# Compressed attention in chains of two token blocks, with its values laid out once by transfers

## The chip, the cores and the metric

The kernel runs on one core of a Trainium2 chip. The core has a matrix engine (TensorE: PE in the profile, PEld for its weight loads), VectorE (DVE), ScalarE (ACT), GpSimd (POOL) and SyncE (SP, which here only issues transfers). The metric is the device time of one execution in microseconds (us), and the median of several runs is quoted.

## The reference, cut to what matters

The model is a two-layer decoder trunk on 512 tokens. Layer A holds a "native sparse attention" of 12 query heads in 3 groups of 4; the heads of a group share keys and values. Three branches are summed with sigmoid gates: compressed blocks, selected blocks and a sliding window. With 512 tokens every allowed block is selected, so the last two branches are ordinary causal attention with two sets of keys. The change is in the compressed branch:

```
def compress(t, i):                       # 31 blocks of 32 tokens, one every 16
    tb = (t[:, :, blk_tok] + cmp_pos[i]).reshape(B, G, n_cmp, CMP_BLOCK * D)
    return gelu(tb @ cmp_w1[i] + cmp_b1[i]) @ cmp_w2[i] + cmp_b2[i]

k_c = rope(rmsnorm(compress(split_heads(k_cmp, G), 0), k_norm[0]), cmp_end)
v_c = compress(split_heads(v_cmp, G), 1)
...
m_c = cmp_end[None, :] <= t[:, None]      # a block counts once it has ended
p_c = masked_softmax(einsum('bgrqd,bgcd->bgrqc', q_b, k_c) * scale, m_c)
o_c = einsum('bgrqc,bgcd->bgrqd', p_c, v_c)
o_c = where(m_c.any(-1)[:, None], o_c, 0) # the first 31 tokens see no block
...
return g_b[..., 0:1] * o_c + g_b[..., 1:2] * o_s + g_b[..., 2:3] * o_w
```

Each query thus has a softmax over at most 31 compressed keys, padded to 32.

## The kernel before, in words

The 512 tokens are 4 blocks of 128, which lie on the 128 partitions. Layer A is `layer_a`. It first makes the projection that feeds the compression and the gates, and the projection of group 0. Then `attend` walks a list of items. An item is one step of attention with a `front` (score products and softmax) and a `back` (transposing the probabilities and multiplying them with the values), and `back` runs one item late. Between items `attend` takes steps from `work`, a queue of other jobs: the compression itself ("cmp"), the projections of groups 1 and 2, the queries, keys and values of the memory attention, and part of the output projection. How many steps are taken for an item is set per group in `RA`. This gives the order in which the program is written; a scheduler then orders the instructions of each engine by that priority and a simulated time, so instructions of neighbouring items are mixed. Each engine runs its own list strictly in order.

Per group there are 16 items of the two causal branches (`attn_a`: front L1041, back L1081) and 4 items of the compressed branch, one for each token block (`cfront`, `cback`, made by `cmp_scores`). `spread` sets where in the list the 4 stand: in group 0 they are items 9 to 12 in one run; in groups 1 and 2 every second item from the second on.

One compressed item is a chain of small instructions:

- four products of queries with the group's compressed keys into a score tile in PSUM (L985);
- on VectorE, adding mask and low part (L990, L991), the row maximum (L993) and its subtraction (L994); the exponential on ScalarE (L995); on VectorE again the sum (L997), the reciprocal (L998) and the product with the gate (L1003, or L1001 for block 0, which also zeroes the first 31 tokens); the product of probabilities and factor on GpSimd (L1004);
- in `back`, one transpose on the matrix engine (L1009) and its copy from PSUM into `pcT` by `evT` (L741 on VectorE or L743 on ScalarE).

When a group's chains are done, `cmp_out` (L1015) adds the compressed branch to the output of a pair of heads with one product of `pcT` and `VCB`. `VCB` is the group's compressed values, 32 rows by 64, repeated at four places of a 128-partition tile that is zero elsewhere: GpSimd clears the tile (L975) and ScalarE makes four copies (L977), for each group anew in a single buffer. The values `vc` themselves come from `finish(1)` in `compress` (L940).

The score tiles of the chain and those of the causal branches (L1050 to L1066, freed when ScalarE's exponentials L226 have read them) share three PSUM banks; transposes share two. The causal items' maxima are L1056 and L1068, their reciprocals L1076, the scaling of probabilities on GpSimd is L735, the copies of transposes L741 and L743, the value products L747. The projections of groups 1 and 2 (`proj_a`) keep all engines busy besides: products L270 to L272, evacuation L955, L958 and L959, rotary embedding on GpSimd (L537 to L540, L759), splitting (L710, L711), transposes (L768, L778) into the tiles that L774 and L716 to L718 write out.

Of the kernel before, what the change touches and what calls it, by code (L numbers as in the profile page):

```python
# [17 lines left out]
NB = 4  # L18
# [25 lines left out]

RA = (2.0, 1.16, 1.46, 1.96)
RB = (1.58, 1.85, 1.49, 2.4, 1.9)


# [130 lines left out]
class K:  # L181
# [602 lines left out]
    def layer_a(self):  # L784
        nc, ins = self.nc, self.ins
        xg = self.xg0
        ab = self.t("ab", [P, 768])
        gt = ab[:, 0:144].rearrange("p (b g) -> p b g", b=NB)
        KC = self.c("KC", [P, 3, 2, 32], F32R)
        vc = ab[0:96, 144:208]  # L790
        raw0, st = [], []

        def evac0(b, ps):
            t = self.t("x", [P, 384])
            nc.scalar.activation(t, ps[:, 0:384], AF.Copy, scale=st[0][:, b : b + 1])
            raw0.append(t)
            nc.scalar.activation(gt[:, b, :], ps[:, 384:420], AF.Copy, scale=st[0][:, b : b + 1])
            if b < NB - 1:
                return
            ga = ab[:, 0:144]  # L800
            nc.vector.tensor_scalar(out=ga, in0=ga, scalar1=-1.0, scalar2=80.0, op0=ALU.mult, op1=ALU.min)
            nc.scalar.activation(ga, ga, AF.Exp)
            nc.vector.tensor_scalar(out=ga, in0=ga, scalar1=1.0, scalar2=None, op0=ALU.add)
            nc.vector.reciprocal(out=ga, in_=ga)

        ga, kf, qm, kk, oT, om = [[] for _ in range(3)], [], [], [], [], []
        x0 = self.x

        def hook(k):
            if k + 1 < KT:  # L810
                self.xpart(k + 1)
            i = self.square(k, x0[k], nc.vector)
            if k == KT // 2:
                self.constants_in(i)
            if k == KT - 1:
                self.setup2()
                st.extend(self.stats_cols())
                self.ms = self.mem_stats()

        self.xpart(0)  # L820
        p0 = self.proj_a(
            0, xg, st, ga[0], banks=[self.pacc] * 2 + [self.pS] * 2, lo="v", fine=True, hook=hook
        )
        for _ in range(KT):
            next(p0)
        drain(weave(p0, self.proj(xg, ins["w_a0"], 420, evac0, lo="g", pool=[self.pS, self.pacc, self.pacc, self.pS]), RC[0]))
        e = st[1]
        hidden, finish = self.compress(raw0, KC, vc)
        cmp = dict(KC=KC, vc=vc)
        work, seen, self.kf1 = Work(), [], []  # L830
        comp = chain(hidden(0, self.pacc), weave(hidden(1, self.pacc), finish(0), RC[1]), finish(1))
        work.add(weave(comp, self.mem_kv_whole(0, kf), RC[2]), "cmp")
        work.add(self.proj_a(1, xg, st, ga[1]), "g1")
        work.add(self.proj_a(2, xg, st, ga[2]), "g2", lambda: seen.count(0) == 20)
        work.add(self.mem_q(0, xg, ins["w_am"], e, qm), None, lambda: seen.count(1) == 20)
        work.add(self.mem_keys(0, kf, kk), "mem")
        work.add(self.mem_kv(1, self.kf1))
        work.add(self.outpart(oT, 0, 4, ins["w_ao"], ins["xT"], 0))
        L, C = zip(*[self.attn_a(g, ga[g], gt, cmp, oT) for g in range(3)])
        M = self.mem_items(kf, qm, kk, om, 3, "mem")  # L840
        items = spread(L[0], C[0], 8, 0) + spread(L[1], C[1], 1, 1) + spread(L[2], C[2], 1, 1) + M
        slow = Work()
        slow.add(paced(self.adds, PA), None, lambda: len(seen) >= 12)
        attend(items, work, slow, RA, seen)
        while work.step() is not END:
            pass
        drain(self.outpart(oT + om, 4, 8, ins["w_ao"], None, 4))

    def compress(self, raw0, KC, vc):

        nc, ins = self.nc, self.ins
        acc = {}
# [34 lines left out]
        def finish(which):  # L887
# [48 lines left out]
            else:  # L936
                ps = self.ps(self.pT, [96, HD])
                for kt in range(2):
                    nc.tensor.matmul(ps, gT[:, kt, :], w2[:, kt, :], start=kt == 0, stop=kt == 1)
                nc.vector.tensor_tensor(out=vc, in0=ps, in1=b2, op=ALU.add)  # L940
            yield
        return hidden, finish

# [25 lines left out]
    def cmp_scores(self, g, q4, cmp, gt):  # L969


        nc = self.nc
        KC, vc = cmp["KC"], cmp["vc"]
        VCB = self.t("vcb", [P, 2, P])
        nc.gpsimd.memset(VCB, 0.0)  # L975
        for q in range(4):
            nc.scalar.activation(  # L977
                VCB[32 * q : 32 * q + 32, q // 2, (q % 2) * HD : (q % 2 + 1) * HD], vc[32 * g : 32 * g + 32, :], AF.Copy
            )
        pcT = self.t("x", [P, S])  # L980

        def front(i):
            Sc = self.ps(self.pS, [P, 4, 2, 32])
            for h in range(4):
                nc.tensor.matmul(  # L985
                    Sc[:, h].rearrange("p t c -> p (t c)"), q4[h // 2][:, h % 2, i * P : (i + 1) * P],
                    KC[:, g].rearrange("p t c -> p (t c)"), start=True, stop=True,
                )
            s = self.t("cs", [P, 4, 32])
            nc.vector.tensor_tensor(out=s, in0=Sc[:, :, 0], in1=bcast(self.ccm[:, i, :], 1, 4), op=ALU.add)  # L990
            nc.vector.tensor_tensor(out=s, in0=Sc[:, :, 1], in1=s, op=ALU.add)  # L991
            m = self.t("c1", [P, 4])
            nc.vector.tensor_reduce(out=m, in_=s, axis=AX.X, op=ALU.max)  # L993
            nc.vector.tensor_tensor(out=s, in0=s, in1=bcast(m, 2, 32), op=ALU.subtract)  # L994
            nc.scalar.activation(s, s, AF.Exp)  # L995
            z = self.t("c2", [P, 4])
            nc.vector.tensor_reduce(out=z, in_=s, axis=AX.X, op=ALU.add)  # L997
            nc.vector.reciprocal(out=z, in_=z)  # L998
            gc = gt[:, i, :].rearrange("p (h b) -> p h b", b=3)[:, 4 * g : 4 * g + 4, 0]
            if i == 0:  # L1000
                nc.vector.scalar_tensor_tensor(out=z, in0=z, scalar=self.zc, in1=gc, op0=ALU.mult, op1=ALU.mult)  # L1001
            else:
                nc.vector.tensor_tensor(out=z, in0=z, in1=gc, op=ALU.mult)  # L1003
            nc.gpsimd.tensor_tensor(out=s, in0=s, in1=bcast(z, 2, 32), op=ALU.mult)  # L1004
            return s

        def back(i, s):
            pt = self.ps(self.pT, [P, P])
            nc.tensor.transpose(pt, s.rearrange("p h c -> p (h c)"), self.idf)  # L1009
            self.evT(pcT[:, i * P : (i + 1) * P], pt)  # L1010

        return VCB, pcT, front, back

# [6 lines left out]
    def attn_a(self, g, ga, gt, cmp, out):  # L1020
# [9 lines left out]

        def cback(i, s):
            cs[3](i, s)
            if i == NB - 1:
                cs.append(True)
                close()

# [44 lines left out]
        def back(pr, half, hp, ii, p):  # L1081
# [40 lines left out]
        need = f"g{g}" if g else None  # L1122
        return (
            [Item(front, back, a, g, need) for a in order],
            [Item(cfront, cback, (i,), g, "cmp") for i in range(NB)],
        )

    def outpart(self, oT, k0, k1, wsrc, xsrc, w0, wide=1):
# [692 lines left out]
```

## Time and profile before

| | |
|---|---|
| median of 3 runs | 1273.14 us (1271.8 to 1274.15) |
| the profiled execution: time, span | 1268.89 us, 1267.1 us |
| granted TensorE clock | 0.998 of full speed |
| busy share of the span | PE 98%, PEld 80%, DVE 66%, ACT 59%, POOL 27% |
| instructions | PE 6416, DVE 1516, ACT 1668, POOL 448 |
| chains of the compressed branch | 12, from 105.99 us (first L985) to 244.9 us (last L1009) |

The span is what the profile covers; the time lies 1.79 us above it. A line number stands for the line of the kernel that issued the instruction, and can be that of a helper. In a row of the timeline the first number is the start and the second the duration in us; a bracket at the end gives the idle time of the engine just before and the instruction that ended it.

### The profile page before, as it was taken

How to read it: one execution, taken by the hardware profiler on the slowest of the kernel's cores; microseconds unless marked ns; L12 is line 12 of the kernel's file. 1: busy time of each engine (PE TensorE's matmuls, PEld its weight loads, DVE VectorE, ACT ScalarE, POOL GpSimd, SP SyncE). 2: the span in 40 equal slices, each digit the busy share in tenths (PEclk: the TensorE clock that was granted, in tenths of full speed). 3: DMA queues.
4: the chain of work that ended last, by engine and by line, in shares of the span. 5: the costliest groups of instructions: out<-in, count | busy, mean ns of one | idle time of the engine just before them, and what ended most of it. 6: DMA issues, size and time to landing. Idle time of an engine off the chain costs nothing.

```text
span 1267.1 us, 18289 instructions
## 1 busy us (share of the span) xinstructions
PE 1238.2 (98%) x6416; PEld 1019.6 (80%) x6416; DVE 835.9 (66%) x1516; ACT 750.7 (59%) x1668; POOL 343.1 (27%) x448
## 2 busy tenths in 40 slices
PE   9999989899999999999999999999999999999998
PEld 7768777677788888888888898987788888888887
DVE  6846676755656557566579567787766756656566
ACT  6845578774575364453647457788666445364462
POOL 4546675632040010000002788552222000000000
PEclk9999999999999999999999999999999999999999
DMA  7531241335488697896976331210459789696534
GB/s 266 198 112 65 68 132 61 67 76 135 157 250 239 225 274 220 268 242 216 282 205 190 120 101 58 63 47 9 117 190 277 220 271 241 219 279 204 164 102 164
DMA packets 61835, 215.26 MB, mean 170 GB/s; under 512 B 6736, under 2 KB 14928, under 8 KB 61232
## 3 DMA queue, kind: packets, MB, share of 16 engines
q1 hardware_dynamic: 50656, 143.69, 34.2%
q0 software_dynamic: 9344, 35.77, 14.2%
q10 hardware_dynamic: 1744, 34.63, 7.6%
q8 instruction: 51, 0.84, 0.3%
q14 instruction: 40, 0.33, 0.1%
HBM read 208.83 MB, written 72.35 MB: 222 GB/s over the span
## 4 chain that ended last, share of the span: by engine, by line
PE 80%; DVE 7%; ACT 7%; POOL 2%; issue 2%; DMA 2%; ACTq 0%; POOLq 0%; DVEq 0%
PE s_ps L270 13%; PE s_ps L271 13%; PE s_ps L272 13%; PE s_acc L270 6%; PE s_acc L271 6%; PE s_acc L272 6%; PE s_po L747 3%; PE s_pt L270 3%; PE s_pt L272 3%; PE s_pt L271 3%; ACT s_p L226 1%; DVE s_w L265 1%; PE s_acc L880 1%; PE s_acc L579 1%; PE s_pt L1100 1%
## 5 line engine op out<-in xcount | busy, mean ns | idle before, releaser
L265 DVE TENSOR_TENSOR s_w<-s_st,s_w 128x1024 fp32r<-128x1024 f32 (+3 forms) x254 | 291.0, 1151 | 260.5 <-ACT s_w L263 250.8
L263 ACT ACTIVATE s_w<-s_st 128x1024 fp32r<-128x1024 f32 (+4 forms) x260 | 251.5, 970 | 182.4 <-PE s_pt L272 45.9
L270 PE MATMUL s_ps<-s_act,s_w 128*128 128x512 f32 x568 | 222.0, 393 | 1.1 <-ACT s_act L305 0.7
L271 PE MATMUL s_ps<-s_act,s_w 128*128 128x512 f32 x568 | 221.1, 390 | 0.0
L272 PE MATMUL s_ps<-s_act,s_w 128*128 128x512 f32 x568 | 221.0, 390 | 0.0
L270 PEld LDWEIGHTS s_ps<-s_act,s_w 128*128 128x128 f32 x568 | 106.5, 188 | 24.4 <-ACT s_act L305 1.6
L271 PEld LDWEIGHTS s_ps<-s_act,s_w 128*128 128x128 f32 x568 | 106.7, 188 | 22.9 <-issue 0.8
L272 PEld LDWEIGHTS s_ps<-s_act,s_w 128*128 128x128 f32 x568 | 106.6, 188 | 22.1
L226 ACT ACTIVATE s_p<-s_ps 128x512 f32<-128x512 f32 x64 | 38.2, 598 | 117.9 <-PE s_ps L272 117.1
L270 PE MATMUL s_acc<-s_w,s_act 128*128 128x512 f32 (+3 forms) x288 | 101.4, 357 | 2.3 <-ACT s_sq L518 1.5
L271 PE MATMUL s_acc<-s_w,s_act 128*128 128x512 f32 (+3 forms) x288 | 101.2, 354 | 0.2 <-DVE s_w L265 0.2
L272 PE MATMUL s_acc<-s_w,s_act 128*128 128x512 f32 (+3 forms) x288 | 100.4, 354 | 0.0
L1183 POOL DMA_DIRECT2D sum<-in_w_db_dram x16 | 14.4, 900 | 291.1 <-ACT s_p L226 287.5
L735 POOL TENSOR_SCALAR s_p<-s_p,s_cr,s_ab 128x128 f32<-128x128 f32 (+3 forms) x96 | 61.1, 673 | 55.3 <-DVE s_cr L1076 28.5
L226 ACT ACTIVATE s_p<-s_ps,s_nm 128x256 f32<-128x256 f32 (+3 forms) x128 | 65.6, 523 | 16.4 <-DVE s_nm L726 5.0
L270 PEld LDWEIGHTS s_acc<-s_w,s_act 128*128 128x128 f32 x288 | 54.7, 190 | 8.7 <-ACT s_sq L518 2.5
L743 ACT ACTIVATE s_pt<-s_pt 128x512 f32<-128x512 f32 (+2 forms) x101 | 53.0, 528 | 13.6 <-PE s_pt L1100 6.0
L305 ACT ACTIVATE s_qk<-s_p 128x256 fp32r<-128x256 f32 (+1 forms) x96 | 46.9, 489 | 21.1 <-DVE s_p L1193 19.2
L271 PEld LDWEIGHTS s_acc<-s_w,s_act 128*128 128x128 f32 x288 | 54.8, 190 | 4.7 <-DVE s_w L265 0.4
L272 PEld LDWEIGHTS s_acc<-s_w,s_act 128*128 128x128 f32 x288 | 54.7, 190 | 4.3
L1183 POOL DMA_DIRECT2D sum<-sum x16 | 14.1, 883 | 151.0 <-issue 39.2
L308 DVE TENSOR_TENSOR s_qk<-s_p,s_qk 128x256 fp32r<-128x256 f32 (+1 forms) x96 | 50.0, 520 | 0.7 <-ACT s_qk L305 0.6
(332 smaller groups left out, 2869.3 us busy)
## 6 DMA issues: line engine op xcount, KB each, us to landing
s_st<-in_w_up_dram SPq DMA_DIRECT2D x64, 512.0 KB, 4.3
s_st<-sum SPq DMA_DIRECT2D x64, 512.0 KB, 6.7
s_st<-in_w_db_dram SPq DMA_DIRECT2D x48, 512.0 KB, 4.5
sum<-in_w_db_dram POOLq DMA_DIRECT2D x16, 1024.0 KB, 14.1
sum<-sum POOLq DMA_DIRECT2D x16, 1024.0 KB, 11.0
s_st<-in_w_bq_dram SPq DMA_DIRECT2D x16, 384.0 KB, 3.1
s_st<-in_w_ag_dram SPq DMA_DIRECT2D x11, 512.0 KB, 3.4
s_w<-in_w_c_dram SPq DMA_DIRECT2D x8, 512.0 KB, 4.4
```

The source lines that it names most:

```text
L226: return lambda *a, **k: self.marks.append(f(*a, **k))
L263: nc.scalar.activation(w[:, 0], st, AF.Copy)
L265: e.tensor_tensor(out=w[:, 1], in0=st, in1=w[:, 0], op=ALU.subtract)
L270: mm(ps, lh[0], rh[0], start=start, stop=False, skip_group_check=again)
L271: mm(ps, lh[0], rh[1], start=False, stop=False, skip_group_check=again)
L272: mm(ps, lh[1], rh[0], start=False, stop=stop, skip_group_check=again)
L305: nc.scalar.activation(dst[:, 0], src, AF.Copy)
L308: nc.vector.tensor_tensor(out=dst[:, 1], in0=src, in1=dst[:, 0], op=ALU.subtract)
L735: self.nc.gpsimd.tensor_scalar(out=p, in0=p, scalar1=c, scalar2=g, op0=ALU.mult, op1=ALU.mult)
L743: self.turned = self.nc.scalar.activation(dst, src, AF.Copy)
L747: i = self.nc.tensor.matmul(*a, **k)
L1183: self.behind(self.nc.gpsimd.dma_start(t[o], x, accum_op=ALU.add, max_dma_last_dim=4096))
```

## The change

1. A chain takes two token blocks: 2 chains per group in place of 4. Its score tile is [128, 2, 4, 2, 32], 512 numbers wide (a whole PSUM bank), and each VectorE, ScalarE and GpSimd instruction of the chain covers 256 columns, not 128. The products (now 8 per chain) and the transposes (2 per chain, into one PSUM tile) stay as many in all; the copy into `pcT` is one for two blocks.
2. The zeroing of the first 31 tokens moves from each group's first chain to the gates, in one instruction for all groups.
3. `VCB` holds all three groups. It is cleared once, and right behind `vc` in `finish(1)` twelve small transfers, issued by GpSimd, write the values to their places. The four copies per group on ScalarE and the clearing per group go.
4. Items and ratios: there are 18 items per group, no longer 20, so `RA` is raised to take about as many steps of work per group, the thresholds that start two jobs become 18, and the chains of groups 1 and 2 stand as every third item.
5. `VCB` (three times as large) and the wider chain tiles take more SBUF; the area reserved for GpSimd's transfer descriptors is set to 8192 bytes, which had been left at the default.

```diff
-RA = (2.0, 1.16, 1.46, 1.96)
+RA = (2.22, 1.29, 1.62, 1.96)
...
             nc.vector.reciprocal(out=ga, in_=ga)
+            g0 = gt[:, 0, :].rearrange("p (h k) -> p h k", k=3)[:, :, 0]
+            nc.vector.tensor_scalar(out=g0, in0=g0, scalar1=self.zc, scalar2=None, op0=ALU.mult)
...
-        hidden, finish = self.compress(raw0, KC, vc)
-        cmp = dict(KC=KC, vc=vc)
+        VCB = self.t("vcb", [P, 3, 2, P])
+        nc.gpsimd.memset(VCB, 0.0)
+        hidden, finish = self.compress(raw0, KC, vc, VCB)
+        cmp = dict(KC=KC, VCB=VCB)
...
-        work.add(self.proj_a(2, xg, st, ga[2]), "g2", lambda: seen.count(0) == 20)
-        work.add(self.mem_q(0, xg, ins["w_am"], e, qm), None, lambda: seen.count(1) == 20)
+        work.add(self.proj_a(2, xg, st, ga[2]), "g2", lambda: seen.count(0) == 18)
+        work.add(self.mem_q(0, xg, ins["w_am"], e, qm), None, lambda: seen.count(1) == 18)
...
-        items = spread(L[0], C[0], 8, 0) + spread(L[1], C[1], 1, 1) + spread(L[2], C[2], 1, 1) + M
+        items = spread(L[0], C[0], 8, 0) + spread(L[1], C[1], 1, 2) + spread(L[2], C[2], 1, 2) + M
...
                 nc.vector.tensor_tensor(out=vc, in0=ps, in1=b2, op=ALU.add)
+                for g in range(3):
+                    for q in range(4):
+                        d = VCB[32 * q : 32 * q + 32, g, q // 2, (q % 2) * HD : (q % 2 + 1) * HD]
+                        s_ = vc[32 * g : 32 * g + 32, :]
+                        nc.gpsimd.dma_start(d, s_)
...
-        KC, vc = cmp["KC"], cmp["vc"]
-        VCB = self.t("vcb", [P, 2, P])
-        nc.gpsimd.memset(VCB, 0.0)
-        for q in range(4):
-            nc.scalar.activation(
-                VCB[32 * q : 32 * q + 32, q // 2, (q % 2) * HD : (q % 2 + 1) * HD], vc[32 * g : 32 * g + 32, :], AF.Copy
-            )
+        KC = cmp["KC"]
+        VCB = cmp["VCB"][:, g]
         pcT = self.t("x", [P, S])

         def front(i):
-            Sc = self.ps(self.pS, [P, 4, 2, 32])
-            for h in range(4):
...
+            Sc = self.ps(self.pS, [P, 2, 4, 2, 32])
+            for b in range(2):
+                blk = slice((2 * i + b) * P, (2 * i + b + 1) * P)
+                for h in range(4):
+                    nc.tensor.matmul(
+                        Sc[:, b, h].rearrange("p t c -> p (t c)"), q4[h // 2][:, h % 2, blk],
+                        KC[:, g].rearrange("p t c -> p (t c)"), start=True, stop=True,
+                    )
+            s = self.t("cs", [P, 2, 4, 32])
+            nc.vector.tensor_tensor(out=s, in0=Sc[:, :, :, 0], in1=bcast(self.ccm[:, 2 * i : 2 * i + 2], 2, 4), op=ALU.add)
+            nc.vector.tensor_tensor(out=s, in0=Sc[:, :, :, 1], in1=s, op=ALU.add)
...
-            if i == 0:
-                nc.vector.scalar_tensor_tensor(out=z, in0=z, scalar=self.zc, in1=gc, op0=ALU.mult, op1=ALU.mult)
-            else:
-                nc.vector.tensor_tensor(out=z, in0=z, in1=gc, op=ALU.mult)
-            nc.gpsimd.tensor_tensor(out=s, in0=s, in1=bcast(z, 2, 32), op=ALU.mult)
+            nc.vector.tensor_tensor(out=z, in0=z, in1=gc, op=ALU.mult)
+            nc.gpsimd.tensor_tensor(out=s, in0=s, in1=bcast(z, 3, 32), op=ALU.mult)
             return s

         def back(i, s):
-            pt = self.ps(self.pT, [P, P])
-            nc.tensor.transpose(pt, s.rearrange("p h c -> p (h c)"), self.idf)
-            self.evT(pcT[:, i * P : (i + 1) * P], pt)
+            pt = self.ps(self.pT, [P, 2, P])
+            for b in range(2):
+                nc.tensor.transpose(pt[:, b], s[:, b].rearrange("p h c -> p (h c)"), self.idf)
+            self.evT(pcT[:, 2 * i * P : (2 * i + 2) * P].rearrange("p (b q) -> p b q", b=2), pt)
...
-            if i == NB - 1:
+            if i == NB // 2 - 1:
...
-            [Item(cfront, cback, (i,), g, "cmp") for i in range(NB)],
+            [Item(cfront, cback, (i,), g, "cmp") for i in range(NB // 2)],
...
-    nc = bacc.Bacc("TRN2", target_bir_lowering=False, num_devices=1)
+    nc = bacc.Bacc("TRN2", target_bir_lowering=False, num_devices=1, dynamic_dma_scratch_size=8192)
```

More of the change, by code (lines that the diff above doesn't have):

```diff
@@ L847, in layer_a, with compress @@
         drain(self.outpart(oT + om, 4, 8, ins["w_ao"], None, 4))
-    def compress(self, raw0, KC, vc):
+    def compress(self, raw0, KC, vc, VCB):
         nc, ins = self.nc, self.ins
@@ L972, in cmp_scores @@
         nc = self.nc
-        KC, vc = cmp["KC"], cmp["vc"]
-        VCB = self.t("vcb", [P, 2, P])
-        nc.gpsimd.memset(VCB, 0.0)
-        for q in range(4):
-            nc.scalar.activation(
-                VCB[32 * q : 32 * q + 32, q // 2, (q % 2) * HD : (q % 2 + 1) * HD], vc[32 * g : 32 * g + 32, :], AF.Copy
-            )
+        KC = cmp["KC"]
+        VCB = cmp["VCB"][:, g]
         pcT = self.t("x", [P, S])
         def front(i):
-            Sc = self.ps(self.pS, [P, 4, 2, 32])
-            for h in range(4):
[L985 to L992, printed above, removed]
+            Sc = self.ps(self.pS, [P, 2, 4, 2, 32])
[9 more added lines that the diff above has]
+            nc.vector.tensor_tensor(out=s, in0=Sc[:, :, :, 1], in1=s, op=ALU.add)
+            m = self.t("c1", [P, 2, 4])
@@ L993, in front @@
             nc.vector.tensor_reduce(out=m, in_=s, axis=AX.X, op=ALU.max)
-            nc.vector.tensor_tensor(out=s, in0=s, in1=bcast(m, 2, 32), op=ALU.subtract)
+            nc.vector.tensor_tensor(out=s, in0=s, in1=bcast(m, 3, 32), op=ALU.subtract)
             nc.scalar.activation(s, s, AF.Exp)
-            z = self.t("c2", [P, 4])
+            z = self.t("c2", [P, 2, 4])
             nc.vector.tensor_reduce(out=z, in_=s, axis=AX.X, op=ALU.add)
             nc.vector.reciprocal(out=z, in_=z)
-            gc = gt[:, i, :].rearrange("p (h b) -> p h b", b=3)[:, 4 * g : 4 * g + 4, 0]
@@ L1000, in front @@
-            if i == 0:
-                nc.vector.scalar_tensor_tensor(out=z, in0=z, scalar=self.zc, in1=gc, op0=ALU.mult, op1=ALU.mult)
-            else:
-                nc.vector.tensor_tensor(out=z, in0=z, in1=gc, op=ALU.mult)
-            nc.gpsimd.tensor_tensor(out=s, in0=s, in1=bcast(z, 2, 32), op=ALU.mult)
+            gc = gt[:, 2 * i : 2 * i + 2, :].rearrange("p b (h k) -> p b h k", k=3)[:, :, 4 * g : 4 * g + 4, 0]
+            nc.vector.tensor_tensor(out=z, in0=z, in1=gc, op=ALU.mult)
```

## The prediction

> **What bounds the kernel now.** I read the page's busy shares first, then the busy time in three stretches (before, in and behind the part where the compressed chains of groups 1 and 2 run), then the matrix engine's own gaps in the timeline of that part.
>
> ```profile
> span 1267.1 us, 18289 instructions
> PE 1238.2 (98%) x6416; PEld 1019.6 (80%) x6416; DVE 835.9 (66%) x1516; ACT 750.7 (59%) x1668; POOL 343.1 (27%) x448
> ...
> core 0: us, PE busy (x) PEld busy (x) DVE busy (x) ACT busy (x) POOL busy (x), PEclk, DMA share, GB/s
> 0.00:150.00 150.00, 145.16 (x718) 112.04 (x719) 98.48 (x226) 89.45 (x240) 78.22 (x119) 1.00 0.43 150
> 150.00:280.00 130.00, 117.25 (x819) 93.05 (x819) 91.53 (x235) 100.80 (x308) 73.96 (x106) 1.00 0.31 82
> 280.00:1267.10 987.10, 975.83 (x4882) 814.51 (x4878) 645.86 (x1057) 560.48 (x1121) 190.97 (x226) 1.00 0.62 185
> 117.00:140.00 23.00, 23.00 (x132) 18.30 (x131) 16.05 (x31) 14.31 (x37) 17.36 (x19) 1.00 0.30 92
> ```
>
> The matrix engine is the bound: 98% busy, idle for 28.9 us in all. The change takes no work from it (as many products and transposes), so it can only win from those gaps, and 130.00 - 117.25 = 12.75 us of them lie between 150 and 280 us. There ScalarE is busy for 100.80 of 130 us and VectorE for 91.53: the causal softmax passes through both, in order, and anything put into their queues holds scores or transposes back. From 117 to 140 us, where group 0's chains run and the transfers will be issued, the matrix engine has no gap at all (23.00 of 23.00): projections fill it. These are the gaps that I put down to the compressed chains:
>
> ```profile
> 171.61 0.70 PE L1052 MATMUL s_ps<-s_qk,s_qk 128*128 128x512 f32 x2 [0.84 <-DVE s_cs L991]
> 185.11 0.62 PE L1065 MATMUL s_ps<-s_qk,s_qk 128*128 128x384 f32 x2 [0.36 <-DVE s_cs L991]
> 187.48 0.74 PE L1065 MATMUL s_ps<-s_qk,s_qk 128*128 128x512 f32 x2 [1.04 <-ACT s_p L226]
> 189.26 0.73 PE L1065 MATMUL s_ps<-s_qk,s_qk 128*128 128x512 f32 x2 [0.31 <-DVE s_cs L991]
> 198.32 0.55 PE L1100 MATMUL s_pt<-c,s_p 128*128 128x128 f32 x3 [0.37 <-ACT s_x L743]
> 208.63 0.73 PE L1065 MATMUL s_ps<-s_qk,s_qk 128*128 128x512 f32 x2 [1.21 <-ACT s_p L226]
> 228.20 0.63 PE L1100 MATMUL s_pt<-c,s_p 128*128 128x128 f32 x4 [1.30 <-DVE s_pt L741]
> 237.96 0.30 PE L1009 MATMUL s_pt<-c,s_cs 128*128 128x128 f32 x1 [0.78 <-ACT s_pt L743]
> 239.78 0.73 PE L1065 MATMUL s_ps<-s_qk,s_qk 128*128 128x512 f32 x2 [0.93 <-ACT s_p L226]
> ...
> 226.15 1.43 DVE L994 TENSOR_TENSOR s_cs<-s_cs,s_c 128x128 f32<-128x128 f32 x1
> 227.51 0.54 DVE L741 COPY s_pt<-s_pt 128x384 f32<-128x384 f32 x1
> 225.50 2.78 POOL L735 TENSOR_SCALAR s_p<-s_p,s_cr,s_ab 128x512 f32<-128x512 f32 x4
> 184.16 1.06 ACT L977 ACTIVATE s_vcb<-s_ab 32x64 f32<-32x64 f32 x4
> 236.14 1.05 ACT L977 ACTIVATE s_vcb<-s_ab 32x64 f32<-32x64 f32 x4
> ```
>
> Three kinds are to be seen. The causal scores wait for a PSUM bank that a chain still holds until L991: 0.84 + 0.36 + 0.31 = 1.51 us. One wait of 1.30 us is for a copy (L741) that stood behind an L994 of 1.43 us, while GpSimd ran L735 beside it. And ScalarE is late, for 1.04, 0.78 and 0.93 us, two to four us behind the start of a group's four copies L977, with 0.37 us for a chain's own transpose copy (L743 into s_x). That is 1.51 + 1.30 + 2.75 + 0.37 = 5.93 us. The 1.21 us at 208.63 stands near no chain.
>
> **The change part by part.** The durations of a chain:
>
> ```profile
> L990 DVE TENSOR_TENSOR s_cs<-s_ps,c x12: 229/280/292, 106.6 to 238.3; 128x128 f32<-128x128 f32 x12
> ...
> L994 DVE TENSOR_TENSOR s_cs<-s_cs,s_c x12: 266/291/1434, 108.4 to 240.0; 128x128 f32<-128x128 f32 x12
> L995 ACT ACTIVATE s_cs<-s_cs x12: 293/310/333, 108.7 to 240.4; 128x128 f32<-128x128 f32 x12
> L1003 DVE TENSOR_TENSOR s_c<-s_c,s_ab x9: 142/196/837, 114.4 to 243.2; 128x4 f32<-128x4 f32 x9
> L1004 POOL TENSOR_TENSOR s_cs<-s_cs,s_c x12: 393/400/405, 112.1 to 243.6; 128x128 f32<-128x128 f32 x12
> 150.00:280.00 130.00, 2.29 (x8) 1.12 (x8) 12.30 (x40) 2.49 (x8) 3.21 (x8) 1.00 0.31 82
> L1056 DVE TENSOR_REDUCE s_nm<-s_ps 128x2 f32<-128x256 f32 x10 | 4.1, 414 | 0.1
> L305 ACT ACTIVATE s_x<-s_p x32: 401/418/420, 367.3 to 1231.9; 128x256 fp32r<-128x256 f32 x32
> L649 POOL TENSOR_TENSOR s_tq<-s_act,gr x2: 727/735/743, 239.3 to 246.5; 128x256 f32<-128x256 f32 x2
> ```
>
> VectorE: the chain's five wide instructions take 12.30 us between 150 and 280 us (40 of them, for the tile s_cs; the stretch row here is that tile's alone). With 256 columns I take L1056's 0.414 us; 4 chains x 5 x 0.414 = 8.3 us, 4.0 us less. The narrow ones (L1003: 0.196 us, 0.837 at worst) halve in number, with some 1.5 us. ScalarE: two groups' copies, 1.06 + 1.05 = 2.1 us, go; the exponentials, 2.49 us, become 4 x 0.418 = 1.7; evictions halve and widen. So about 3 of ScalarE's 100.80 us. GpSimd: 8 x 0.400 become 4 x 0.735, 0.3 us less, and the clearing per group goes. In group 0 the same is saved by halves, and worth nothing while the matrix engine has no gap there; should that cover go, it is a gain, not a loss.
>
> What this is worth on the matrix engine, gap by gap. *Banks* (1.51 us): half as many chains, each with two adds of 0.414 for 0.28, so I take half: -0.75. *L994 beside GpSimd* (1.30): half as many instructions that can collide: -0.65; nothing at worst, all at best. *Copies* (2.75): the 1.06 us goes from ScalarE's queue, but in these microseconds it also waits for the other engines, so I take a little over half: -1.5, between 0 and -2.75. *Transpose copies* (0.37): -0.2. In sum -3.1 us; all gone would be -5.9, and with the 1.21 us at 208.63, which a less loaded ScalarE may shorten, -7.1.
>
> The transfers are the new cost, and they stand in GpSimd's queue behind a wait for `vc`:
>
> ```profile
> L940 DVE TENSOR_TENSOR s_ab<-s_pt,gr x1: 220/220/220, 116.8 to 116.8; 96x64 f32<-96x64 f32 x1
> L912 POOL DMA_DIRECT2D s_tmp<-in_w_c_dram x2: 559/572/584, 83.5 to 110.3; - x2
> DMA to landing us min/median/max: 2.0/2.0/2.0
> L1183 POOL DMA_DIRECT2D sum<-in_w_db_dram x16: 872/881/997, 224.8 to 1122.6; - x16
> 126.66 0.41 DVE L958 TENSOR_TENSOR s_tq<-s_acc,gr 128x256 f32<-128x256 f32 x1
> 138.58 0.42 DVE L958 TENSOR_TENSOR s_tq<-s_acc,gr 128x256 f32<-128x256 f32 x1
> 149.53 1.07 PE L1015 MATMUL s_po<-s_x,s_vcb 128*128 128x512 f32 x2
> L1009 PEldq EVENT_SEMAPHORE  x9: 51/51/696, 126.3 to 243.4; - x9
> L975 POOL MEMSET s_vcb<- x3: 312/312/313, 0.9 to 235.4; 128x256 f32 x3
> 228.59 0.61 PE L985 MATMUL s_ps<-KC,s_qk 128*128 128x64 f32 x4
> ```
>
> At L912's 0.572 us twelve issues take 6.9 us, at L1183's longest (0.997) 12.0; I take the first, since L912 is the nearer in size (64 KB against 1 MB). They stand ahead of group 1's rotary embedding (L537 to L759) from 117 us on. What waits behind that: the tile of the next projection block (L958 at 126.66), so its PSUM bank comes free that much later. The next-but-one block ended at 138.58 and needs that bank only then or later, so GpSimd can be late by about 138.58 - 126.66 = 11.9 us before the matrix engine feels it: 6.9 us cost nothing, 12.0 us about 0.1. The values must be there at 149.53; 116.8 + 6.9 + 2.0 = 125.7 us, 24 us early. For its L1015 the matrix engine now looks at the semaphores of several transfers, long over, in place of ScalarE's; the nearest row is an extra semaphore instruction of 0.051 us (L1009, PEldq), so +0.1 us in all, between 0 and 12 x 0.051 = 0.6. I put the extra gate instruction at the 0.196 us of L1003, hidden behind filled products; clearing 768 columns once, at L975's rate 3 x 0.312 = 0.9 us, depends on nothing and can run as early as that row's first, at 0.9 us. If these had no cover they would cost 0.2 and 0.9 us.
>
> Against the transfers speaks a rule of the Trainium skill, "SBUF — State Buffer", section "SBUF: two separate sides": while VectorE runs a copy in its two-port mode, GpSimd cannot write the descriptors of a transfer, and one of about 620 ns takes about 3100. By that, twelve would be estimated at up to 12 x 3.1 = 37 us of GpSimd, and the sum would turn into a loss; no run shows it yet, and L912 measured 0.559 and 0.584.
>
> The smaller descriptor area: the sixteen summing transfers of L1183's row start one per (1122.6 - 224.8) / 15 = 60 us (as many more of the other kind lie between), so few are ever under way together. I put it at nothing; if it made GpSimd wait, the down projections would get their sums late, and that would show as waits for transfers behind 280 us. Ratios and thresholds keep the steps per group (2.0 x 20 = 40.0 against 2.22 x 18 = 40.0), so the filling work is the same; the new order of instructions may move gaps either way by the size of one, +-1 us.
>
> Sum: -3.1 + 0.1 = -3.0 us on the profiled execution: 1268.89 - 3.0 = 1265.9. The median of the runs is 4.25 us above that execution, so 1270.1 us is what I expect of the runs.
>
> **The rivals.**
> *More comes back:* all 5.9 to 7.1 us of gaps, since a lighter queue shortens the rest too: 1273.1 - 6.5 = 1266.6. For it: ScalarE's 78% load. Against: 12.75 - 5.93 = 6.8 us of the stretch's gaps stand away from any chain.
> *Hidden:* gaps move instead of closing, since the causal softmax (L226 to L735 to the transpose) is as long as before and the matrix engine waits for that next: 1272.6. For it speaks the 1.21 us at 208.63 without a chain nearby.
> *Slower by the bank:* a double chain holds one of three score banks through 8 products and two wide adds. Four L985 took 0.61 us, so the bank is held some 0.61 + 2 x (0.414 - 0.28) = 0.9 us longer. If each of the 4 double chains of groups 1 and 2 makes the scores wait 0.9 + 0.84 (the longest seen) = 1.74 us, that is 7.0 us in place of 1.51, or +5.5, and with the other terms (-2.25) +3.2: 1276.3. It decides from (2.25 + 1.51) / 4 = 0.94 us of wait per double chain on. Against it: 8 chains made only three such waits.
> *Slower by GpSimd:* each issue takes 2.6 us (0.572 and the landing's 2.0) because it waits for the one before or for VectorE. 31 us less the 11.9 us of margin, with the products of other groups to fill half: about +9, 1282. Against it: L912's rows. The rule of the Trainium skill's "SBUF — State Buffer" above would give it a cause.
>
> **How the numbers follow.** Forecast (-1.5 to -4.5 us) 0.50; more comes back 0.14; hidden 0.14; slower by the bank 0.14; slower by GpSimd or its descriptors 0.08. About 0.2%, 2.5 us, is what a measurement can tell from no change; of the forecast's 0.50 I count 0.32 beyond it. So faster 0.32 + 0.14 = 0.46, same 0.18 + 0.14 = 0.32, slower 0.22. The range runs from all gaps gone, 1273.1 - 7.1 = 1266.0, to a little past the bank's rival, 1276.5; the forecast's own is 1268.6 to 1271.6.
>
> **What would show it.** Right: no L977; L990 to L997 near 0.41 us, six each; between 150 and 280 us ScalarE about 3 us and VectorE 5 us below before and the matrix engine's gaps near 10 us; POOL issues near 0.57 us each from about 117 us. Wrong: waits of score products for L991 over 0.94 us per chain; POOL issues of 1 us and more with gaps between 125 and 150 us; gaps in the stretch still 12 us or more.

## The result, and the profile after

| | before | after |
|---|---|---|
| median of 4 runs beside each other | 1272.77 us (1271.8 to 1274.15) | 1259.01 us (1258.24 to 1259.37) |
| ratio, 95% interval | | 0.989 [0.9873, 0.9907] |
| profiled execution: time, span | 1268.89, 1267.1 us | 1259.13, 1257.4 us |

The change takes 13.8 us off the median, where 3.0 were forecast. Between the two profiled executions it is 9.7 us of span; where the other 4 us are is told further down (the granted clock).

The busy shares and the three stretches of the kernel after, in the views shown of before (in the second, the stretch and its length, then busy time and instructions of PE, PEld, DVE, ACT, POOL, then granted clock, DMA share, GB/s):

```profile
span 1257.4 us, 18253 instructions
PE 1235.4 (98%) x6416; PEld 1019.2 (81%) x6416; DVE 831.6 (66%) x1475; ACT 745.8 (59%) x1644; POOL 343.0 (27%) x452
```

```profile
0.00:150.00 150.00, 144.74 (x718) 111.60 (x719) 101.51 (x221) 89.47 (x237) 81.83 (x129) 1.00 0.41 143
150.00:280.00 130.00, 125.43 (x895) 103.08 (x894) 87.41 (x217) 102.37 (x316) 77.51 (x111) 1.00 0.34 92
280.00:1257.00 977.00, 965.19 (x4806) 804.49 (x4805) 642.69 (x1037) 554.01 (x1093) 183.70 (x213) 1.00 0.63 186
```

The matrix engine's gaps between 150 and 280 us fall from 130.00 - 117.25 = 12.75 us to 130.00 - 125.43 = 4.57 us. That is 8.2 of the 9.7 us; it now does 895 instructions in that stretch, not 819. Outside it the gaps grow by 1.4 us (0 to 150 us: 4.84 before, 5.26 after; behind 280 us: 11.27 before, 12.21 after). Busy time falls by 2.8 us, from 1238.2 to 1235.4 us for the same 6416 instructions: 8.2 - 1.4 + 2.8 = 9.6, the difference of the spans but for rounding. Its groups, busy time and mean ns, then the idle time before them; before:

```profile
L1100 PE MATMUL s_pt<-c,s_p 128*128 128x128 f32 x168 | 26.7, 277 | 3.2 <-DVE s_pt L741 1.3 <-ACT s_pt L743 0.6 <-POOL s_p L735 0.5
L1065 PE MATMUL s_ps<-s_qk,s_qk 128*128 128x512 f32 x48 | 17.2, 444 | 4.5 <-ACT s_p L226 4.1 <-DVE s_cs L991 0.3
L1052 PE MATMUL s_ps<-s_qk,s_qk 128*128 128x512 f32 x24 | 8.6, 433 | 1.2 <-DVE s_cs L991 0.8 <-ACT s_p L226 0.3
L985 PE MATMUL s_ps<-KC,s_qk 128*128 128x64 f32 x48 | 7.0, 270 | 0.1
L1009 PE MATMUL s_pt<-c,s_cs 128*128 128x128 f32 x12 | 3.4, 281 | 0.8 <-ACT s_pt L743 0.8
```

and after (lines moved by 4 to 6):

```profile
L1104 PE MATMUL s_pt<-c,s_p 128*128 128x128 f32 x168 | 25.6, 275 | 0.7 <-DVE s_r L520 0.7
L1069 PE MATMUL s_ps<-s_qk,s_qk 128*128 128x512 f32 x48 | 17.2, 441 | 1.7 <-ACT s_p L226 1.4
L1056 PE MATMUL s_ps<-s_qk,s_qk 128*128 128x512 f32 x24 | 8.4, 425 | 0.5 <-ACT s_p L226 0.5
L991 PE MATMUL s_ps<-KC,s_qk 128*128 128x64 f32 x48 | 6.0, 273 | 0.0
L1013 PE MATMUL s_pt<-c,s_cs 128*128 128x128 f32 x12 | 2.3, 277 | 0.3 <-issue 0.2
```

The chain's own 60 instructions lose 2.1 us of busy time and the causal transposes 1.1: they now stand in longer runs of their kind (the 8 products of a chain together, two transposes together). The idle columns show who waited less: the causal scores (4.5 to 1.7, 1.2 to 0.5) and the causal transposes (3.2 to 0.7). Not one wait for the chain's adds is left. Three of the gaps that stay, the longest among them, in the timeline:

```profile
161.07 1.52 PE L747 MATMUL s_po<-s_pt,s_x 128*64 128x256 f32 x16 [0.40 <-ACT s_pt L743]
189.33 1.52 PE L747 MATMUL s_po<-s_pt,s_x 128*64 128x256 f32 x16 [0.41 <-ACT s_pt L743]
215.55 0.52 PE L1104 MATMUL s_pt<-c,s_p 128*128 128x128 f32 x3 [0.74 <-DVE s_r L520]
```

The terms of the new work: the chain's tile (duration min/median/max in ns, first and last start), that tile alone between 150 and 280 us, and the values' tile:

```profile
L996 DVE TENSOR_TENSOR s_cs<-s_ps,c x6: 403/413/424, 109.1 to 222.3; 128x256 f32<-128x256 f32 x6
L1000 DVE TENSOR_TENSOR s_cs<-s_cs,s_c x6: 369/520/747, 112.1 to 224.8; 128x256 f32<-128x256 f32 x6
L1007 POOL TENSOR_TENSOR s_cs<-s_cs,s_c x6: 615/708/899, 116.6 to 228.5; 128x256 f32<-128x256 f32 x6
```

```profile
150.00:280.00 130.00, 1.58 (x8) 0.96 (x8) 8.67 (x20) 1.66 (x4) 2.93 (x4) 1.00 0.34 92
```

```profile
L949 POOL DMA_DIRECT2D s_vcb<-s_ab x12: 496/497/534, 120.0 to 125.5; - x12
DMA to landing us min/median/max: 1.6/2.6/5.5
```

### The profile page after: what moved, and what is told of

The parts are those of the page before. It is cut to its first block, busy times and chain, and to the rows that moved or that the text cites. A ratio compares the mean times of both kernels' runs of the same rounds, so it can differ in the third digit from the quotient of the medians.

```text
span 1257.4 us, 18253 instructions
## 1 busy us (share of the span) xinstructions
PE 1235.4 (98%) x6416; PEld 1019.2 (81%) x6416; DVE 831.6 (66%) x1475; ACT 745.8 (59%) x1644; POOL 343.0 (27%) x452
## 4 chain that ended last, share of the span: by engine, by line
PE 71%; DVE 5%; ACT 4%; DMA 3%; POOL 2%; issue 2%; ACTq 0%; DVEq 0%; POOLq 0%
PE s_ps L270 13%; PE s_ps L271 13%; PE s_ps L272 12%; PE s_acc L270 4%; PE s_acc L272 4%; PE s_acc L271 4%; PE s_pt L270 3%; PE s_pt L272 3%; PE s_pt L271 3%; PE s_po L747 3%; DVE s_w L265 1%; DMA s_st<-in_w_ao_dram 1%; ACT s_p L226 1%; PE s_ps L1560 1%; ACT s_w L263 1%
## 5 line engine op out<-in xcount | busy, mean ns | idle before, releaser
L226 ACT ACTIVATE s_p<-s_ps 128x512 f32<-128x512 f32 x64 | 38.0, 594 | 95.3 <-PE s_ps L272 93.6
L226 ACT ACTIVATE s_p<-s_ps,s_nm 128x256 f32<-128x256 f32 (+3 forms) x128 | 65.7, 529 | 12.1 <-PE s_pt L1098 4.5
L271 PE MATMUL s_acc<-s_w,s_qk 128*128 128x512 f32 x128 | 49.9, 390 | 0.0
```

The costliest lines, as they stand in the source:

```text
L226: return lambda *a, **k: self.marks.append(f(*a, **k))
L271: mm(ps, lh[0], rh[1], start=False, stop=False, skip_group_check=again)
```

## What the trace of before holds that the prediction did not use

Chains and tiles of group 1, before: four products (L985) fill a score bank, L990 reads it into the tile `cs`, and the transpose L1009 sets that tile free. There are two such tiles.

```profile
175.57 0.53 PE L985 MATMUL s_ps<-KC,s_qk 128*128 128x64 f32 x4
176.20 0.28 DVE L990 TENSOR_TENSOR s_cs<-s_ps,c 128x128 f32<-128x128 f32 x1
176.59 0.53 PE L985 MATMUL s_ps<-KC,s_qk 128*128 128x64 f32 x4
177.89 0.50 PE L985 MATMUL s_ps<-KC,s_qk 128*128 128x64 f32 x3
183.34 0.27 PE L1009 MATMUL s_pt<-c,s_cs 128*128 128x128 f32 x1
183.85 0.28 DVE L990 TENSOR_TENSOR s_cs<-s_ps,c 128x128 f32<-128x128 f32 x1
186.14 0.30 PE L1009 MATMUL s_pt<-c,s_cs 128*128 128x128 f32 x1
187.50 0.28 DVE L990 TENSOR_TENSOR s_cs<-s_ps,c 128x128 f32<-128x128 f32 x1
```

The second chain's add follows its products at once. The third's products begin at 176.59, its add at 183.85: it waits until the first chain's transpose (183.34) gives back a tile. The fourth waits from about 177.9 to 187.50. So one bank is held for 7.3 us and another for 9.6 us with scores that nothing reads, and from about 177.9 to 183.85 us both are: for some 6 us the causal scores have one bank of three. Group 2 repeats it (products at 228.59 and 230.08, adds at 235.46 and 238.29). The row of the waits between 150 and 280 us (total, times, longest) is small, because VectorE did other work in the meantime:

```profile
DVE s_cs L990 <- PE s_pt L1009: 2.0, 1, 2.0
```

After the change the same two buffers of `cs` hold two token blocks each, so all four blocks of a group are in them:

```profile
167.03 1.06 PE L991 MATMUL s_ps<-KC,s_qk 128*128 128x64 f32 x8
169.52 0.40 DVE L996 TENSOR_TENSOR s_cs<-s_ps,c 128x256 f32<-128x256 f32 x1
172.24 0.97 PE L991 MATMUL s_ps<-KC,s_qk 128*128 128x64 f32 x8
174.68 0.41 DVE L996 TENSOR_TENSOR s_cs<-s_ps,c 128x256 f32<-128x256 f32 x1
```

My theory was therefore: the gain is the wait for a tile that is gone, not the shorter queues. Rivals: the wide instructions themselves; the transfers; the new order of the filling work. The experiments bear this out only in part: bringing the wait back loses the gain (a1), but taking it away alone brings a third of it (e2) or nothing (s1).

## The experiments

All ratios are to the kernel before on the same chip, with 95% intervals. The scheduler orders each kernel anew, so every edit also shifts instructions; the order's own effect is tested too.

**Parts done alone.** *Area* (before with the smaller descriptor area), *four tiles* (that and `cs=4`), *transfers* (that area, the values by transfers, single chains), *chains* (after, with ScalarE's copies and no transfers).

```diff
# e1: before
+dynamic_dma_scratch_size=8192
# e2: e1 and
-        cs=2, stt=4, vcb=1, ab=1,
+        cs=4, stt=4, vcb=1, ab=1,
# e3: e1, with VCB, memset and the 12 transfers of the change
# e4: after, without them: VCB per group by 4 ACT copies, as before
```

> The kernel before with the descriptor area at 8192 bytes and nothing else; every engine's list of instructions is the same. Every theory expects no change, 1272 to 1274 us. If the area matters (a theory of its own: the timed runs of before lie 4 us above its profiled one, and the summing transfers may be part of that), it shows here as more than 2.5 us.

> The kernel before with four buffers for the chain's score tile (cs) instead of two, and the small descriptor area for room. Held banks (group 0's third and fourth chain wait for a cs buffer from 110 to 131 and 141 us and hold two of three score banks meanwhile; with two double chains nobody waits): most of the gain comes, 1262 to 1266 us, group 0's score products L1065 move from 146 us to about 130, the chains' L990 run close together. Short chains (the prediction's reason: the chains of groups 1 and 2 as such make the gaps): no change, within 2 us of before. Order (any new order of instructions moves the time by several us): either sign.

> The kernel before with only the values' part of the change: VCB for all groups by twelve transfers, four chains per group kept. Short chains: the copies' share of the gaps, 1 to 2.7 us, comes back: 1270 to 1272 us. Held banks: nothing or the same 1 to 2 us. If the transfers alone carry the result: near 1260 us.

> The changed kernel without the values' part: two blocks to a chain, new ratios and spacing, but ScalarE's four copies per group. Short chains and held banks: most of the 13.8 us, 1260 to 1264 us, some 1 to 2.7 us short of the changed kernel. If the transfers carry the result: near 1272 us.

| | median us | ratio |
|---|---|---|
| e1 area | 1270.75 | 1.0001 [0.9989, 1.0013] |
| e2 four tiles | 1266.13 | 0.9967 [0.9956, 0.9978] |
| e3 transfers | 1273.58 | 1.0024 [1.0013, 1.0035] |
| e4 chains | 1260.16 | 0.992 [0.9899, 0.9941] |

The double chains carry the gain; the area does nothing, and the transfers alone cost 3 us with single chains. Four tiles take the wait away (the last three adds of group 1 now follow their products) and win a third, just under what I had expected of the held banks. That e3 would lose time no theory had expected. Kernel e2:

```profile
177.50 0.28 DVE L990 TENSOR_TENSOR s_cs<-s_ps,c 128x128 f32<-128x128 f32 x1
178.67 0.28 DVE L990 TENSOR_TENSOR s_cs<-s_ps,c 128x128 f32<-128x128 f32 x1
179.93 0.28 DVE L990 TENSOR_TENSOR s_cs<-s_ps,c 128x128 f32<-128x128 f32 x1
```

```profile
150.00:280.00 130.00, 120.72 (x842) 96.23 (x841) 90.36 (x236) 103.02 (x316) 74.07 (x106) 1.00 0.31 82
```

The gaps of the stretch are 9.28 us, between before's 12.75 and after's 4.57. Which waits went is seen in the causal scores of the stretch, first before, then e2, and in one gap that e2 keeps:

```profile
L1065 PE MATMUL s_ps<-s_qk,s_qk 128*128 128x512 f32 (+1 forms) x70 | 22.0, 407 | 5.0 <-ACT s_p L226 4.0 <-DVE s_cs L991 0.7
L1065 PE MATMUL s_ps<-s_qk,s_qk 128*128 128x512 f32 (+1 forms) x70 | 22.5, 410 | 1.9 <-ACT s_p L226 1.7
226.93 0.63 PE L1100 MATMUL s_pt<-c,s_p 128*128 128x128 f32 x4 [1.29 <-DVE s_pt L741]
```

The scores' waits fall by 3.1 us, with ScalarE's copies L977 still there (at 185.90 and 234.87 us). The wait for L741 behind a long L994 stays as it was (1.30 us before), and so does the wait for L991 at 172.93 us (0.86, before 0.84): these two have another cause than the tile.

**Where.** The kernel after again, double chains only in group 0, double chains only in groups 1 and 2 (both with ScalarE's copies), and the kernel after with one wide tile, so that the second chain has to wait for the first one's transposes.

```diff
# g0_only, g12_only: after with copies; n = 2 if g in TWO else 1 blocks to a chain
+TWO = (0,)        # g12_only: (1, 2)
# a1_cs1: after
-        cs=2, stt=4, vcb=1, ab=1,
+        cs=1, stt=4, vcb=1, ab=1,
```

> The changed kernel again, on the same chip as the three that follow. All theories: the ratio of 0.989 to before repeats, and the kernel with the chains alone (ratio 0.992) lies 0 to 4 us above it; the transfers' part of the result is that difference.

> Double chains in group 0 alone (with its ratio of 2.22 and its threshold), single ones in groups 1 and 2, ScalarE's copies kept. Held banks: as much as four buffers gave, 4 us below before, ratio 0.996 to 0.998. Short chains: nothing, since the matrix engine has no gap there, ratio 0.999 to 1.001. The chains of all groups give 0.992.

> Double chains in groups 1 and 2 alone, ScalarE's copies kept; group 0's third and fourth chain still wait for one of two cs buffers and hold two score banks. Short chains: 3 to 6 us below before, ratio 0.995 to 0.998, and together with group 0's part the 0.992. Held banks alone: ratio 0.999 to 1.001.

> The changed kernel with one buffer for the chain's score tile in place of two, so that in every group the second chain waits for the first one's transposes while it holds one of three score banks. Held banks: 2 to 5 us of the gain are lost, group 0's second L996 starts at about 134 us and not at 109.85, and the score products of group 0 come later. Short chains: within 2 us of the changed kernel.

| | median us | ratio |
|---|---|---|
| a0 after | 1259.59 | 0.9909 [0.9892, 0.9927] |
| g0 only | 1273.61 | 1.0021 [1.0006, 1.0035] |
| g1 and g2 only | 1264.73 | 0.9946 [0.9929, 0.9964] |
| a1 one tile | 1271.53 | 0.9996 [0.9985, 1.0007] |

Group 0 alone wins nothing, as the full matrix engine there said; its chains too waited for tiles (adds of before at 106.61, 108.15, 131.06 and 140.86 us), and that wait shows no price beside the projections. The held banks, as I had written them down for this run, were to win e2's 4 us in group 0; that was a miss, and the theory from here on speaks of groups 1 and 2 alone. These win more than either theory expected, but e4, double in all groups, is 4.6 us faster still. By 280 us the profiles of both have done as many matrix-engine instructions (1586 and 1585), so that difference arises behind, where no chain runs; why is open. One buffer fewer takes away the whole gain, 12 us where 2 to 5 were expected, with all wide instructions, transfers and ratios in place. Kernel a1, group 1:

```profile
173.29 0.97 PE L991 MATMUL s_ps<-KC,s_qk 128*128 128x64 f32 x8
183.17 0.38 PE L1013 MATMUL s_pt<-c,s_cs 128*128 128x128 f32 x2
183.66 0.42 DVE L996 TENSOR_TENSOR s_cs<-s_ps,c 128x256 f32<-128x256 f32 x1 [2.44 <-PE s_pt L1013]
```

Its second chain holds its bank from 173.29 to 183.66, 10.4 us, as the third and fourth of before did. Between 150 and 280 us its matrix engine is busy for 118.44 us with 820 instructions (before 117.25 with 819), VectorE for 79.30 and ScalarE for 93.44: lighter queues than before's 91.53 and 100.80, and no faster. The granted clock of that stretch was 0.97 in a1 and 1.00 in before, but a1's two runs at a clock of 0.998 took 1268.46 and 1269.19 us, as before's do at that clock. That rules out lighter queues as the cause by themselves. VectorE itself also stands still before that late add (2.44 us, and 3.38 us in group 0), so a1 does not tell the held bank from VectorE's own wait; both come from the missing tile.

**The rest, and the order.** Before with four tiles and the transfers (s1); before with the ratios raised by 3% (o1); after with 3% more (o2); after with chains at every second item (o3).

```diff
# s1: e3 with cs=4
# o1: before
-RA = (2.0, 1.16, 1.46, 1.96)
+RA = (2.06, 1.19, 1.5, 1.96)
# o2: after
-RA = (2.22, 1.29, 1.62, 1.96)
+RA = (2.29, 1.33, 1.67, 1.96)
# o3: after
-spread(L[1], C[1], 1, 2) + spread(L[2], C[2], 1, 2)
+spread(L[1], C[1], 1, 1) + spread(L[2], C[2], 1, 1)
```

> The kernel before with four cs buffers and the values laid out by transfers, but four single chains per group, its own ratios and spacing. Held banks, now for groups 1 and 2 (group 0's hold cost nothing): as the four buffers alone or a little better, ratio 0.994 to 0.997. If the rest of the gain (about 7 us) is the double chain's own, fewer and wider instructions, this kernel stays there; if it is the transfers on top of free banks, ratio 0.991.

> The kernel before with ratios raised by 3% for groups 0 to 2 (2.06, 1.19, 1.5) and nothing else, a measure of what another order of the same instructions does. Held banks: the hold stays, ratio 0.998 to 1.003. Order as the cause of the result: 4 us or more either way, down to 0.992.

> The changed kernel with ratios raised by 3% (2.29, 1.33, 1.67). Held banks and short chains: no hold comes back, so the gain stays, ratio 0.988 to 0.994 to before. Order as the cause: the gain is mostly lost.

> The changed kernel with the chains of groups 1 and 2 as every second item from the second on, as before, so that their two chains stand closer together. Held banks and short chains: the gain stays, ratio 0.989 to 0.994. Order: mostly lost.

| | median us | ratio |
|---|---|---|
| s1 single, four tiles, transfers | 1273.1 | 1.0014 [1.0004, 1.0024] |
| o1 before, ratios +3% | 1269.6 | 0.9985 [0.9975, 0.9995] |
| o2 after, ratios +3% | 1256.74 | 0.9887 [0.9869, 0.9904] |
| o3 after, spacing of before | 1259.44 | 0.991 [0.9886, 0.9935] |

These orders move a kernel by 0 to 3 us and do not mix the two kinds. s1 was a miss: with four tiles it should have kept e2's gain, and it lost it. So the free tile alone is not enough. The profiles of s1 and e3 share what e2's has not: a gap of the matrix engine of 1.98 and 1.91 us (at 213.01 and 212.47 us; e2's longest there is 1.11 us), and then a granted clock of 0.57 from 213 to 217 us. Why the transfers bring that gap to single chains is not shown.

**What else a double chain has.** From the kernel after, one thing undone each time: softmax instructions for one block each (n1); a PSUM tile and a copy for each transpose (n2); a score bank for each block (n3); the ratios of before (r1). Then ratios raised by 6% (o4), and four wide tiles (w4, area at 4096 bytes).

```diff
# n1: all of L996 to L1007 per block, on s[:, b], 128 columns
# n2: per block
+                pt = self.ps(self.pT, [P, P])
# n3: per block, with its own two adds into s[:, b]
+                Sc = self.ps(self.pS, [P, 4, 2, 32])
# r1: RA = (2.0, 1.16, 1.46, 1.96); o4: RA = (2.36, 1.37, 1.72, 1.96)
# w4: cs=4, dynamic_dma_scratch_size=4096
```

> The kernel after with items of two blocks, one score tile (one bank) and one tile of 256 columns per chain as they are, but every VectorE, ScalarE and GpSimd instruction of the softmax issued for one block (128 columns), as before. If the win is that VectorE, ScalarE and GpSimd have less to do, the ratio to before goes back to about 0.996 (VectorE gets its 4 to 5 us between 150 and 280 us back, and the bank is held for four adds of 0.28 us in place of two of 0.41). If the win is that no chain waits for a tile with a bank in its hands, and that the products come in one run, it stays at 0.989 to 0.993.

> The kernel after, but each block's transpose in a PSUM tile of its own with a copy of its own (12 copies of 128 columns in place of 6 of 256). If the pairs of transposes carry part of the win, the ratio rises from 0.990 to 0.993 or more; if they do not, it stays at 0.989 to 0.992.

> The kernel after, but each block's score products in a bank of its own, added by two instructions of 128 columns into the halves of one wide tile; from the maximum on all is as after. The tile is asked for before the first product, and one buffer serves both blocks. If banks taken twice as often are what costs, the ratio rises to 0.994 or more; if the wait for a tile of two buffers is what costs, it stays at 0.989 to 0.993, because a chain still needs one tile for two blocks.

> The kernel after with the ratios of before (2.0, 1.16, 1.46). The order of the work moves single kernels by 2 to 3 us: 0.987 to 0.993, on the same side as the other kernels with double chains. If the ratios were part of the win, it would lie at 0.994 or more.

> The kernel after with the three ratios raised by another 6% (2.36, 1.37, 1.72), so that work is drawn still earlier. With the ratios of before the ratio was 0.994, with those of after 0.9896, with 3% more 0.9887. If earlier filling goes on paying, 0.986 to 0.988; if the filling work now runs out for the last items of group 2, 0.990 or more, with new gaps behind 230 us.

> The kernel after with four buffers of the wide tile in place of two (the descriptor area at 4096 bytes makes the room). With two buffers, two chains per group and one group at a time, no chain waits for a tile any more: if the wait for the tile is what the buffers decide, nothing changes, 0.988 to 0.991. Under 0.987 would say that a wait for the tile is left.

| | median us | ratio |
|---|---|---|
| n1 narrow softmax | 1262.25 | 0.9929 [0.9909, 0.995] |
| n2 transposes apart | 1264.34 | 0.9948 [0.9931, 0.9964] |
| n3 bank per block | 1264.73 | 0.995 [0.9933, 0.9966] |
| r1 old ratios | 1263.65 | 0.994 [0.9916, 0.9963] |
| o4 ratios +6% | 1258.36 | 0.9899 [0.9876, 0.9922] |
| w4 four wide tiles | 1259.67 | 0.9912 [0.9893, 0.9931] |

w4 changes nothing: two wide tiles already end the wait. Beside after's 0.989 and 0.9909, PSUM buffers taken twice as often, be it for transposes (n2) or scores (n3), cost 4 to 6 points of a thousand, some 5 us; their intervals lie above both of after's ([0.9873, 0.9907] and [0.9892, 0.9927]). The old ratios (r1) cost 3 to 5 points, with an interval that overlaps after's second; one gap of the matrix engine in r1, behind a late copy, is longer than any of after's between 150 and 280 us:

```profile
175.99 0.63 PE L1104 MATMUL s_pt<-c,s_p 128*128 128x128 f32 x4 [1.73 <-DVE s_pt L741]
```

The narrow instructions (n1) cost 2 to 4 points; their interval overlaps most of after's second, so a price for the width is not shown. The parts do not add up: one tile fewer costs 12 us, e2's two tiles more win 4, and n2, n3 and r1 lose some 4 to 5 each.

## The granted clock

The forecast put the 4.25 us between the profiled execution and the median on top of the sum as a constant. It is none. In the 78 runs of the kernel before beside the experiments, time goes with the granted clock of the run (correlation -0.86, 0.83 us for 0.001): the 15 runs at 0.998 or above have a median of 1268.7 us (1268.04 to 1269.68), the 18 at 0.994 or below 1273.0. The profiled execution was one of the former. The four runs of after all have 0.998 or 0.999, and so do a0, e4, g12, o2 to o4 and w4 (0.998 to 1.0). At equal clock the change is worth 1268.7 - 1259.0 = 9.7 us, which is the difference of the spans; the other 4 us of the median go with the clock, which was under 0.998 in 63 of the 78 runs of before. Kernel e1 has before's instructions in before's order; its profiled execution shows one such loss. Windows of 4 us, first of before, then of e1 (the second number is the matrix engine's busy time, the clock is the third from the end):

```profile
184.00:188.00 4.00, 2.45 (x17) 1.87 (x16) 3.96 (x12) 3.47 (x12) 0.00 (x0) 1.00 0.02 4
188.00:192.00 4.00, 3.63 (x25) 3.04 (x25) 4.00 (x14) 3.66 (x11) 1.71 (x3) 1.00 0.77 262
184.00:188.00 4.00, 2.46 (x16) 1.85 (x15) 4.00 (x12) 3.47 (x12) 0.00 (x0) 0.99 0.01 4
188.00:192.00 4.00, 3.94 (x18) 3.29 (x17) 3.62 (x13) 3.26 (x11) 1.70 (x3) 0.58 0.73 262
```

In a1's profile a longer one is seen whole (windows of 2 us):

```profile
186.00:188.00 2.00, 1.63 (x12) 1.30 (x10) 2.00 (x6) 1.43 (x4) 1.08 (x2) 1.00 0.00 0
188.00:190.00 2.00, 1.36 (x6) 0.97 (x6) 2.00 (x7) 1.94 (x7) 0.23 (x1) 1.00 0.04 8
190.00:192.00 2.00, 0.49 (x2) 0.49 (x3) 2.00 (x7) 0.72 (x2) 1.52 (x2) 0.70 0.00 0
192.00:194.00 2.00, 2.00 (x11) 2.00 (x11) 0.96 (x5) 0.80 (x3) 0.89 (x2) 0.50 0.00 0
194.00:196.00 2.00, 2.00 (x12) 2.00 (x11) 0.00 (x0) 0.00 (x0) 0.34 (x1) 0.50 0.00 0
196.00:198.00 2.00, 2.00 (x12) 1.84 (x11) 0.42 (x1) 0.00 (x0) 0.00 (x0) 0.60 0.00 0
```

From 186 to 192 us the matrix engine is busy for 3.48 of 6 us, while VectorE, busy for 6.00 of 6, has the late chain among its work; then the clock is at 0.50 for some 6 us, with the matrix engine busy throughout. The longest single gap there is 1.56 us:

```profile
191.51 0.58 PE L270 MATMUL s_acc<-s_w,s_act 128*128 128x256 f32 x1 [1.56 <-ACT s_sq L518]
```

So thin filling over some microseconds can be followed by a spell at half speed, and gaps then cost more than their length. It need not be: from 184 to 188 us before and e1 are equally thin (2.45 and 2.46 us of 4), and the clock fell in e1 alone. What decides it no run here shows. Between 150 and 280 us the profiles of a1, e1, e3, n3, o1, r1 and s1 have a mean clock of 0.96 to 0.99, the others 1.00. The Trainium skill, "TensorE: Matmul & The Clock Gate", sections "HAM oscillation — how this bites in real kernels" and "A second HAM failure mode: psum-queue depth-cycling", names idle gaps above about 3.4 us, and in the second case frequent short ones, as what throttles; here only the second fits.

## Why the prediction was wrong in size

Right: the sign; the place (8.2 us of gaps between 150 and 280 us, and nothing from group 0 alone); the area (e1); the transfers beside double chains, at 0.497 us an issue, all issued by 126 us, with no matrix-engine wait for them (after against e4: 1259.0 to 1259.6 and 1260.16), so the rival of slow issues fell away. The rule of the Trainium skill's "SBUF — State Buffer", section "SBUF: two separate sides", found no stall to apply to (0.496 to 0.534 us an issue); whether VectorE ran a copy in its two-port mode meanwhile, no view here shows. The chain's own terms came out: VectorE 8.67 us for the 8.3 forecast, ScalarE 1.66 for 1.7, GpSimd 2.93 for 2.94. VectorE's total in the stretch fell by 4.1 us and ScalarE's rose by 1.6, both with more of the kernel's work in it; the forecast of "ScalarE about 3 us" below before did not allow for work that moves in.

Wrong, by size:

- *Copies, "a little over half: -1.5", and banks, "so I take half: -0.75".* This is the step that failed. It put each gap down to what stood beside it: the waits for L226 to ScalarE's copies, and to a bank only the gaps whose releaser is L991, at the time of products and adds, 0.9 us. But a bank was held for 7 to 10 us by a chain that waited for a tile, and the price appeared as waits for L226. With the tiles alone (e2, copies in place) the causal scores' waits fell from 5.0 to 1.9 us, and the stretch's gaps by 3.5. That the wide tiles double the token blocks in flight was in the change's first and fifth points, and was read as space.
- *"6.8 us of the stretch's gaps stand away from any chain"*, at nothing, and half of the chains' 5.93: the gaps fell by 8.2 us, more than all that was tied to chains. The tile wait by itself accounts for 3.5 of this (e2). The other 4.7 came with the rest of the double chain; n2, n3 and r1 each give 4 to 5 us of the time back, and how they share it is open.
- *L994 beside GpSimd, "half as many instructions that can collide"*: the wait for L741 is in e2 as before, so it is not the tile's. It is gone in after, but in n1 too, which has as many such instructions as before; that halving them closed it is not shown.
- *The bank's rival* had the sign wrong for the same reason: it compared holds of 1 us. No matrix-engine wait of after is for the chain's adds; only with one tile (a1) is the bank held for long, and then before's time comes back (1271.53 us).
- *"The change takes no work from it"*: true by count, but busy time fell by 2.8 us with the longer runs.
- *"+-1 us" for the order*: the ratios of before would have cost about 4 us in the medians (r1 against after), and 3% more moved each kernel by 1.5 to 3 us. Part of the gain may thus be the luck of a good order, which no run tells apart.
- *The 4.25 us offset*: see the clock; about 4 us of the 11.1 by which the median was missed.

"More comes back" (1266.6) was nearest, but it gave a lighter queue as its reason, which a1 speaks against, and was capped at the gaps tied to chains and the one at 208.63 us. What stays open: why transfers with single chains lose 3 us (e3) and s1 all of e2's 4, while beside double chains they cost nothing; and how the 8 us between e2 and after divide between PSUM buffers, ratios and width, as these do not add.

The best version measured is o2, 1256.74 us, 0.9887 [0.9869, 0.9904]; its lead on the kernel after lies within the intervals, and o4 shows that raising the ratios further brings no more.

## What to carry to other kernels

Before pricing a wait on a shared PSUM bank, follow one chain from its first product to the instruction that frees the bank, and look at what that one waits for: a small SBUF tile with two buffers kept a bank held for 7 to 10 us at a time. A tile made twice as wide with the same number of buffers doubles what is in flight. A run with fewer buffers and one with more show what the buffers are worth: here one fewer cost all of the gain, and two more won a third of it, so the rest of the change mattered too. The profiled execution and the median can differ by the clock, and then a change that fills gaps can move the offset too.

## What was unexpected of the hardware

The granted clock went to 0.50 for about 6 us with no gap of the matrix engine above 1.56 us just before it (a1), and the same thin stretch of the same instructions was followed by such a spell in one execution (e1) and not in another (before). The times of before's runs (1268.04 to 1274.81 us) go with the mean granted clock; that spells of this kind make up their spread is likely, but the profiles show single executions only. Twelve small transfers issued back to back by GpSimd took 0.497 us each (median) beside a VectorE that was busy for 5.05 of the 6 us from 120 to 126 us, less than the 0.572 us of the larger transfer that the forecast used.
